# A search for a threshold: two small ScalarE operations of each step become one VectorE operation

## The chip, the cores and the metric

The kernel runs on one core of a Trainium2 chip. Five engines work side by side, each through its own queue in order: TensorE (PE, with its weight loads shown as PEld), VectorE (DVE), ScalarE (ACT), GpSimd (POOL) and SyncE (SP), which issues DMAs. An engine waits for another through semaphores; while the instruction at the head of a queue waits, everything behind it in that queue waits too. The metric is the device time of one execution in microseconds. Three runs of the kernel before gave 1814.0, 1814.33 and 1814.47 us; the median is 1814.33 us.

## What is computed

One transformer block over 1024 positions and a width of 1024: a mixer of two kinds of attention, a cross attention to a memory of 256 positions, and an MLP with a squared ReLU. The first kind of attention picks, for every query, the 256 keys with the largest index score, and attends only to these:

```python
idx_score = jnp.einsum('bqhs,bqh->bqs',
                       jax.nn.relu(jnp.einsum('bqhd,bsd->bqhs', qi, k_i)), wi).astype(jnp.float32)
idx_score = jnp.where(pos[None, None, :] <= t[None, :, None], idx_score, -jnp.inf)
_, sel = lax.top_k(idx_score, k_dsa)
kg = k_d[bidx3, sel]
vg = v_d[bidx3, sel]
s = jnp.einsum('bqhd,bqkd->bhqk', qd, kg).astype(jnp.float32) * ATTN_SCALE
p = _masked_softmax(s, (sel <= t[None, :, None])[:, None])
```

The second kind has three branches (compressed blocks, selected blocks, a sliding window), which are weighted by gates and summed. Everything behind the attention is dense: an output projection, the cross attention, and `square(relu(h @ w_ff_in)) @ w_ff_out`.

## The kernel before

The 1024 queries are eight tiles of 128. The first four tiles are projected alone. Then the attention of the eight tiles runs beside a stream of other work that keeps PE busy: the projection of the other four tiles, the memory's keys and values, and the output projection, cross attention and MLP of tiles that are ready. The last part, from about 1260 us, is the output side of the last tiles alone. `together` and `beside` interleave the generators by the estimated work that each yields; after that a scheduler of the tile framework puts the instructions of each engine in order by a timeline of its own and adds the semaphores. So the order on a queue isn't the order of the source, and an edit in one place can move instructions in others.

For tiles 2 to 7 (tiles 0 and 1 have no more than 256 keys) `index_mask` works one tile ahead of the attention. It computes the index scores (PE, with ReLU on ACT, L604, and the weighted sum on DVE, L608 and L610), and then looks for the 256th largest score of each query, which is each of the 128 partitions' own search. The scores' bits are mapped to two 16-bit halves, `hi` and `lo` (L618 to L620), whose order is that of the scores. The search goes bit by bit: 16 steps over `hi`, then 16 over `lo`, 32 steps a tile and 192 in all. A step of the kernel before has three instructions, all on ACT:

- L636: the sign of (key + threshold) for all keys of the row, 384 to 1024 wide by tile, with the sum of the signs written out to `over`. In the profile this is an ACTIVATE and an ACTIVATION_READ_ACCUMULATOR.
- L637: the sign of `over + need` for the one column, which tells if too many keys lie above the threshold.
- L638: the new threshold, `c - 0.5 * 2^b * step`, again one column.

Each needs the one before. As all three stand on the same engine, no other engine takes part in a step; the scheduler puts other ACT work between them. Between the halves DVE counts the keys above and zeroes the others (L631 to L634), and behind the search DVE rebuilds the threshold and writes the mask (L642 to L655), a chain of about ten instructions, the largest over the whole row. The mask `dmask` is what the score evictions of the first kind of attention add (L678).

Other lines that matter below: L235 (ACT) and L236 (DVE) copy a PSUM tile out in a rounded high part and the rest (`ph`, `pl`, `qh`, `ql`, `h`); L678 (DVE) evicts scores with the mask and the row's minimum `mn`; L680 (ACT) is the exponential; L685 (POOL) scales it; L244 (ACT) and L249 (POOL or DVE) split a weight tile from DRAM into `whi` and `wlo`; L401 (ACT) stages projected queries in `st`; L218 is every matmul of this form. In the changed file the lines from L642 on stand 2 lower down.

Of the kernel before, what the change touches and what calls it, by code (L numbers as in the profile page):

```python
# [9 lines left out]
F32 = mybir.dt.float32  # L10
# [6 lines left out]
AF = mybir.ActivationFunctionType  # L17
ALU = mybir.AluOpType
# [4 lines left out]
P = 128  # L23
# [5 lines left out]
BIG = 1e30  # L29
TOPK = 256  # L30
# [136 lines left out]
def build(nc, tc, I, C, out):  # L167
    v, s, g, te = nc.vector, nc.scalar, nc.gpsimd, nc.tensor
# [7 lines left out]
    at = at_pool.__enter__()  # L176
# [4 lines left out]
    def pst(tag, shape):  # L181
        return psum["pool"].tile(shape, F32, tag=tag, name="ps" + tag, bufs=psum["n"][tag],
                                 padded_shape=[P, 512 // int(np.prod(shape[2:]))] + list(shape[2:]))
# [33 lines left out]
    def mm(o, a, b, start, stop):  # L217
        te.matmul(o, a, b, start=start, stop=stop)  # L218

    def small(pool, tag, w, dt=F32, bufs=2, p=P):  # L220
        return pool.tile([p, w], dt, tag=tag, name=tag, bufs=bufs)
# [364 lines left out]
    def chunks_of(n):  # L586
        if n <= 4:
            return [(0, n)]
        a = (n + 1) // 2
        return [(0, a), (a, n - a)]  # L590

    def index_mask(aw, st, t):
        Wd = (t + 1) * P
        acc = small(aw, "isc", L, bufs=1)
        for hg in range(2):
            qh, ql = q_prep(aw, t, 2, hg)
            for h in range(4):
                for c, n in chunks_of(t + 1):
                    sp = pst("S", [P, n * P])
                    mv = st["K"][:, IDX, c * P:(c + n) * P]  # L600
                    mm(sp, qh[:, h, :], mv, True, False)
                    mm(sp, ql[:, h, :], mv, False, True)
                    r = small(aw, "ir", 512)
                    s.activation(r[:, :n * P], sp, AF.Relu)  # L604
                    dst = acc[:, c * P:(c + n) * P]
                    w = st["wi"][:, t, hg * 4 + h:hg * 4 + h + 1]
                    if hg == 0 and h == 0:
                        v.tensor_scalar(dst, r[:, :n * P], w, None, op0=ALU.mult)  # L608
                    else:
                        v.scalar_tensor_tensor(dst, r[:, :n * P], w, dst, op0=ALU.mult, op1=ALU.add)  # L610
                yield 0.15 * (t + 1)
        sc = acc[:, :Wd]
        v.tensor_tensor(acc[:, t * P:Wd], acc[:, t * P:Wd], causal[:, 384:512], op=ALU.subtract)
        bits = sc.bitcast(I16).rearrange("p (n b) -> p n b", b=2)
        mask = small(aw, "dmask", L, BF16)[:, :Wd]
        sgn = mask.bitcast(I16)
        hi, lo = small(aw, "tkh", L, U16, 1)[:, :Wd], small(aw, "tkl", L, U16, 1)[:, :Wd]
        v.tensor_scalar(sgn, bits[:, :, 1], 0.0, -1.0, op0=ALU.is_lt, op1=ALU.mult)  # L618
        v.scalar_tensor_tensor(hi.bitcast(I16), sgn, -32768, bits[:, :, 1], op0=ALU.bitwise_or, op1=ALU.bitwise_xor)
        v.tensor_tensor(lo.bitcast(I16), bits[:, :, 0], sgn, op=ALU.bitwise_xor)  # L620


        cnt, low = small(aw, "tkc", 1), small(aw, "tkf", 1)
        over, step, need = small(aw, "tko", 1), small(aw, "tks", 1), small(aw, "tkg", 2)
        th = small(aw, "tkt", 2)
        v.memset(need[:, 0:1], Wd - 2 * TOPK + 1.0)
        v.memset(th, 0.5 - 32768.0)
        for half, src in enumerate((hi, lo)):
            c, nd = th[:, half:half + 1], need[:, half:half + 1]
            if half == 1:  # L630
                v.tensor_scalar(low, th[:, 0:1], -1.0, None, op0=ALU.mult)  # L631
                v.tensor_scalar(mask, hi, low, None, op0=ALU.is_gt, op1=ALU.add, accum_out=cnt)
                v.tensor_scalar(nd, cnt, 2.0, Wd - 2 * TOPK + 1.0, op0=ALU.mult, op1=ALU.add)
                v.scalar_tensor_tensor(lo, hi, low, lo, op0=ALU.is_equal, op1=ALU.mult)  # L634
            for b in range(15, -1, -1):
                s.activation(mask, src, AF.Sign, bias=c, accum_out=over)  # L636
                s.activation(step, over, AF.Sign, bias=nd)  # L637
                s.activation(c, step, AF.Identity, scale=-0.5 * (1 << b), bias=c)  # L638
                yield 0.1
        ti = small(aw, "tki", 2, U32)  # L640
        tm, tb = small(aw, "tkm", 1, I32), small(aw, "tkb", 1, U32)
        v.tensor_scalar(ti, th, -1.0, None, op0=ALU.mult)  # L642
        v.scalar_tensor_tensor(tb, ti[:, 0:1], 16, ti[:, 1:2], op0=ALU.logical_shift_left, op1=ALU.bitwise_or)
        v.tensor_scalar(tm, tb.bitcast(I32), 31, None, op0=ALU.arith_shift_right)
        v.tensor_scalar(tm, tm, -1, -2147483648, op0=ALU.bitwise_xor, op1=ALU.bitwise_or)
        v.tensor_tensor(tb, tb, tm.bitcast(U32), op=ALU.bitwise_xor)
        thf = tb.bitcast(F32)
        eq = hi.bitcast(BF16)
        v.tensor_scalar(mask, sc, thf, None, op0=ALU.is_gt, op1=ALU.add, accum_out=cnt)
        v.tensor_scalar(cnt, cnt, -1.0, float(TOPK), op0=ALU.mult, op1=ALU.add)  # L650
        v.tensor_scalar(eq, sc, thf, None, op0=ALU.is_equal)
        v.tensor_tensor_scan(sc, eq, eq, 0.0, op0=ALU.add, op1=ALU.bypass)
        v.scalar_tensor_tensor(eq, sc, cnt[:, 0:1], eq, op0=ALU.is_le, op1=ALU.mult)
        v.tensor_tensor(mask, mask, eq, op=ALU.add)
        v.tensor_scalar(mask, mask, 1.0, -BIG, op0=ALU.subtract, op1=ALU.mult)  # L655
        st["dm"][t] = mask
        yield 0.1
# [169 lines left out]
    def attend(aw, st):  # L827

        main = attention(aw, st)
        held = []  # L830

        def of_tile(t):
            while True:
                x = held.pop() if held else next(main, None)
                if x is None:
                    return
                if x[0] > t:
                    held.append(x)
                    return
                yield x[1]  # L840
        for t in range(NT):
            if t + 1 in [a for a, _ in PARTS[1:]]:
                yield t, None
            side = index_mask(aw, st, t + 1) if 2 <= t + 1 < NT else iter(())
            for w in beside(of_tile(t), tile_work(t), side, 8 * 0.15 * (t + 2) + 3.4):
                yield t, w
        for x in main:
            yield x
# [204 lines left out]
    def pe_stack():  # L1053
# [10 lines left out]
    st = {  # L1064
        "K": at.tile([P, 6, L], F32R, tag="K", name="K"),
        "V": [at.tile([P, NT, 2, 2, 64], F32R, tag=f"V{b}", name=f"V{b}") for b in range(2)],
        "Vd": at.tile([P, NT, 2, 64], F32R, tag="Vd", name="Vd"),
        "Kc": {},
        "Vc": {},
        "cT": [at.tile([64, 2, 64], F32, tag=f"cT{kv}", name=f"cT{kv}") for kv in range(2)],  # L1070
        "cb": [at.tile([64, 1], F32, tag=f"cb{kv}", name=f"cb{kv}") for kv in range(2)],
        "wi": at.tile([P, NT, 8], F32, tag="wi", name="wi"),
        "gi": at.tile([P, NT, 24], F32, tag="gi", name="gi"),
        "dm": {},
        "ix": set(),
    }
    for kv in range(2):
        v.memset(st["cT"][kv], 0.0)
    pe = pe_stack()
# [8 lines left out]
    aw = aw_pool.__enter__()  # L1088
# [54 lines left out]
```

## Time and profile before

| | us |
|---|---|
| median of three runs | 1814.33 |
| the profiled execution's own time | 1807.76 |
| its span, first to last instruction | 1806.0 |
| PE busy | 1700.2 (94%) |
| PE weight loads busy | 1447.8 (80%) |
| DVE busy | 927.8 (51%) |
| ACT busy | 1061.9 (59%) |
| POOL busy | 887.4 (49%) |
| mean granted TensorE clock | 0.976 |
| L636 busy, with its read-out | 84.3 + 84.3 + 18.3 + 18.1 |
| L637 and L638 busy | 55.5 and 55.8 |

Busy time counts an engine's instructions from start to end, overlaps once. The ends of matmuls are modelled, so a busy PE isn't PE at its peak. A row of a group reads: line, engine, operation, output<-inputs, shapes, count, then busy us and mean ns of one, then the engine's idle time just before these instructions and who ended it. A wait is put down to the one that came last. A row of the timeline reads: start in us from the span's start, duration in us, engine, line, operation, and in brackets the engine's idle time just before. A row of one line's summary has min/median/max in ns behind the count, and first and last start in us.

The searches lie at 257 to 339, 364 to 441, 498 to 585, 664 to 764, 866 to 972 and 1097 to 1217 us, for tiles 2 to 7.

### The profile page before, as it was taken

The page shows a single profiled execution, that of the slowest core. Times are in us where ns is not written, and L with a number is a line of the kernel's source. Part 1 is how long each engine was busy: PE and PEld are TensorE (multiplying, and loading weights), DVE is VectorE, ACT ScalarE, POOL GpSimd, SP SyncE. Part 2 cuts the span into 40 slices and gives each one's busy share as a digit, 9 for nine tenths or more (in the row PEclk, how much of TensorE's full clock was granted, in tenths as well). Part 3 has the DMA queues.
Part 4 walks back from the last instruction along what each step waited for, and adds up shares of the span by engine and source line. Part 5 has one row for each costly group of instructions (what it writes and reads, how often), then busy time and mean ns, then how long its engine had stood idle before and what let it go on. Part 6 is the DMA issues. An engine that isn't in the chain of part 4 may idle for free. (4 is left out here: it accounts for less than half of the span.)

```text
span 1806.0 us, 27690 instructions
## 1 busy us (share of the span) xinstructions
PE 1700.2 (94%) x9134; PEld 1447.8 (80%) x9134; DVE 927.8 (51%) x2343; ACT 1061.9 (59%) x2655; POOL 887.4 (49%) x1015
## 2 busy tenths in 40 slices
PE   5987999899989999999998999999999799999998
PEld 5986888688878777788886888888888687787887
DVE  4545757665874776375754555646524322222221
ACT  4445669797688579855896558994513333333332
POOL 2356647363541355568575667662111144545444
PEclk9998999999999999999999999999999799999999
DMA  6235221366336211212122212226384122222222
GB/s 193 73 121 155 70 68 58 114 196 175 102 109 196 87 59 42 75 65 80 59 75 75 62 65 78 65 74 194 98 284 151 47 87 89 97 91 96 94 95 93
DMA packets 171887, 185.38 MB, mean 103 GB/s; under 512 B 26464, under 2 KB 140896, under 8 KB 171744
## 3 DMA queue, kind: packets, MB, share of 16 engines
q1 hardware_dynamic: 163808, 173.13, 30.3%
q0 software_dynamic: 7936, 10.49, 2.2%
q8 instruction: 72, 1.18, 0.3%
q14 instruction: 71, 0.58, 0.1%
HBM read 162.59 MB, written 20.97 MB: 102 GB/s over the span
## 5 line engine op out<-in xcount | busy, mean ns | idle before, releaser
L249 POOL TENSOR_TENSOR wlo<-wraw,whi 128x512 fp32r<-128x512 f32 (+1 forms) x231 | 310.6, 1351 | 280.9 <-ACT whi L244 252.9
L244 ACT ACTIVATE whi<-wraw 128x512 fp32r<-128x512 f32 (+2 forms) x289 | 181.0, 628 | 250.8 <-PE psS L218 156.8
L218 PE MATMUL psD<-whi,xh 128*128 128x256 f32 (+1 forms) x704 | 191.1, 352 | 4.4 <-ACT whi L244 3.4
L218 PE MATMUL psD<-wlo,xh 128*128 128x256 f32 (+1 forms) x704 | 190.3, 352 | 1.6 <-DMA wlo<-in_w_in_dram 1.0
L236 DVE TENSOR_TENSOR pl<-psPT,ph 128x512 fp32r<-128x512 f32 (+1 forms) x232 | 142.1, 621 | 78.9 <-ACT ph L235 76.3
L218 PE MATMUL psD<-whi,h 128*128 128x512 f32 x512 | 174.3, 403 | 3.7 <-ACT whi L244 1.6
L218 PE MATMUL psS<-whi,h 128*128 128x512 f32 x512 | 162.4, 392 | 5.4 <-DVE b L891 5.4
L680 ACT ACTIVATE S<-S,mn 128x128 f32<-128x128 f32 (+7 forms) x192 | 142.7, 744 | 40.5 <-DVE mn L678 39.0
L685 POOL TENSOR_SCALAR S<-S,sums,gi 128x640 f32<-128x640 f32 (+7 forms) x128 | 107.8, 853 | 114.1 <-DVE sums L683 103.5
L235 ACT ACTIVATE ph<-psPT 128x512 fp32r<-128x512 f32 (+1 forms) x232 | 122.9, 540 | 61.5 <-PE psPT L695 57.1
L249 DVE TENSOR_TENSOR wlo<-wraw,whi 128x512 fp32r<-128x512 f32 (+1 forms) x58 | 56.3, 971 | 170.3 <-ACT whi L244 170.1
L218 PEld LDWEIGHTS psD<-wlo,xh 128*128 128x128 f32 x704 | 132.4, 193 | 13.6 <-DMA wlo<-in_w_in_dram 1.4
L218 PEld LDWEIGHTS psD<-whi,xh 128*128 128x128 f32 x704 | 130.0, 193 | 14.2 <-ACT whi L244 3.8
L695 PE MATMUL psPT<-c_ident,S 128*128 128x128 f32 x816 | 131.8, 277 | 3.9 <-POOL S L685 2.6
L891 DVE TENSOR_TENSOR b<-psS,b 128x512 f32<-128x512 f32 (+1 forms) x80 | 49.9, 636 | 138.5 <-PE psS L218 138.5
L218 PE MATMUL psS<-K,qh 128*128 128x384 f32 (+3 forms) x288 | 112.4, 394 | 8.9 <-DVE mn L678 3.9
L218 PEld LDWEIGHTS psS<-whi,h 128*128 128x128 f32 x512 | 96.0, 188 | 30.4 <-DVE b L891 10.1
L218 PEld LDWEIGHTS psD<-whi,h 128*128 128x128 f32 x512 | 95.5, 189 | 25.8 <-ACT whi L244 2.0
L695 PEld LDWEIGHTS psPT<-c_ident,S 128*128 128x128 f32 x816 | 97.6, 142 | 14.1 <-POOL S L685 4.5
L218 PE MATMUL psD<-wlo,h 128*128 128x512 f32 x256 | 102.6, 404 | 1.1 <-POOL wlo L249 1.1
L218 PE MATMUL psD<-xh,wlo 128*128 128x512 f32 x256 | 101.5, 398 | 0.0
L891 DVE TENSOR_TENSOR b<-psD,b 128x512 f32<-128x512 f32 (+1 forms) x112 | 63.2, 573 | 74.0 <-PE psD L218 66.9
(289 smaller groups left out, 4546.2 us busy)
## 6 DMA issues: line engine op xcount, KB each, us to landing
wraw<-in_w_ff_in_dram SPq DMA_DIRECT2D x128, 256.0 KB, 2.7
wraw<-in_w_ff_out_dram SPq DMA_DIRECT2D x128, 256.0 KB, 2.6
whi<-in_w_out_dram SPq DMA_DIRECT2D x32, 256.0 KB, 3.8
wlo<-in_w_out_dram SPq DMA_DIRECT2D x32, 256.0 KB, 4.3
wraw<-in_w_in_dram SPq DMA_DIRECT2D x24, 256.0 KB, 3.4
q<-st SPq DMA_DIRECT2D x12, 512.0 KB, 2.6
qin<-q SPq DMA_DIRECT2D x44, 128.0 KB, 2.3
x<-in_x_dram SPq DMA_DIRECT2D x8, 512.0 KB, 5.5
```

The costliest lines, as they stand in the source:

```text
L218: te.matmul(o, a, b, start=start, stop=stop)
L235: s.activation(hi, src, AF.Copy)
L236: v.tensor_tensor(lo, src, hi, op=ALU.subtract)
L244: s.activation(hi, raw, AF.Copy)
L249: (v if l == "v" else g).tensor_tensor(lo, raw, hi, op=ALU.subtract)
L680: s.activation(S, S, AF.Exp, bias=low, scale=-1.0, accum_out=sums[:, hh:hh + 1])
L685: g.tensor_scalar(Ss[hh], Ss[hh], sums[:, hh:hh + 1], 1.0 if gate is None else gate[:, hh:hh + 1], op0=ALU.mult, op1=ALU.mult)
L695: te.transpose(p2[:, j, hh, :], S[:, (c + j) * P:(c + j + 1) * P], ident)
L891: v.tensor_tensor(dst, pt, dst, op=ALU.add)
```

## The change

L637 and L638 go from ACT, and one DVE instruction, a scalar_tensor_tensor with a sum over its columns written out, takes their place. It works on three columns: `over`, of which the first column is the sum of signs and the two others are a very large number, is compared with `need`, and the 0 or 1 is multiplied with a row of a table `tks` of the step: `-2^b`, the present threshold, and `0.5 * 2^b`. The large numbers always compare as greater, so the sum of the three products is the threshold, plus half of the bit, minus the bit if too many keys lay above. The sum is written to the middle column of the table's next row, from where the next step's L638 (the former L636) takes it as its bias; at the last step it goes to `th`. Table and `over` are now allocated once for the kernel and filled ahead of everything else with 34 column writes on DVE; before, `over`, `step` and `th` were small tiles in rings of two, and `th` was set for each tile.

```diff
-        over, step, need = small(aw, "tko", 1), small(aw, "tks", 1), small(aw, "tkg", 2)
+        over, tks, need = st["tko"], st["tks"], small(aw, "tkg", 2)
         th = small(aw, "tkt", 2)
-        v.memset(need[:, 0:1], Wd - 2 * TOPK + 1.0)
-        v.memset(th, 0.5 - 32768.0)
+        v.memset(need[:, 0:1], 2.0 * TOPK - 1.0 - Wd)
         for half, src in enumerate((hi, lo)):
-            c, nd = th[:, half:half + 1], need[:, half:half + 1]
+            nd = need[:, half:half + 1]
             if half == 1:
                 v.tensor_scalar(low, th[:, 0:1], -1.0, None, op0=ALU.mult)
                 v.tensor_scalar(mask, hi, low, None, op0=ALU.is_gt, op1=ALU.add, accum_out=cnt)
-                v.tensor_scalar(nd, cnt, 2.0, Wd - 2 * TOPK + 1.0, op0=ALU.mult, op1=ALU.add)
+                v.tensor_scalar(nd, cnt, -2.0, 2.0 * TOPK - 1.0 - Wd, op0=ALU.mult, op1=ALU.add)
                 v.scalar_tensor_tensor(lo, hi, low, lo, op0=ALU.is_equal, op1=ALU.mult)
             for b in range(15, -1, -1):
-                s.activation(mask, src, AF.Sign, bias=c, accum_out=over)
-                s.activation(step, over, AF.Sign, bias=nd)
-                s.activation(c, step, AF.Identity, scale=-0.5 * (1 << b), bias=c)
+                i = 15 - b
+                s.activation(mask, src, AF.Sign, bias=tks[:, i, 1:2], accum_out=over[:, 0:1])
+                v.scalar_tensor_tensor(small(aw, "tkj", 3), over, nd, tks[:, i, :], op0=ALU.is_gt, op1=ALU.mult,
+                                       accum_out=tks[:, i + 1, 1:2] if b else th[:, half:half + 1])
                 yield 0.1
...
+    st["tks"] = at.tile([P, 16, 3], F32, tag="tks", name="tks")
+    st["tko"] = at.tile([P, 3], F32, tag="tko", name="tko")
+    v.memset(st["tko"], BIG)
+    v.memset(st["tks"][:, 0, 1:2], 0.5 - 32768.0)
+    for i in range(16):
+        v.memset(st["tks"][:, i, 0:1], -1.0 * (1 << (15 - i)))
+        v.memset(st["tks"][:, i, 2:3], 0.5 * (1 << (15 - i)))
```

## The prediction

> **What bounds the kernel now.** I read the page's engine shares first, then the table of busy time cut at the first and last step of each of the six searches (tiles 2 to 7), then who made TensorE (PE) wait in those stretches.
>
> ```profile
> PE 1700.2 (94%) x9134; PEld 1447.8 (80%) x9134; DVE 927.8 (51%) x2343; ACT 1061.9 (59%) x2655; POOL 887.4 (49%) x1015
> ```
> ```profile
> core 0: us, PE busy (x) PEld busy (x) DVE busy (x) ACT busy (x) POOL busy (x), PEclk, DMA share, GB/s
> 257.00:339.00 82.00, 77.34 (x436) 65.61 (x436) 53.85 (x156) 74.03 (x258) 49.78 (x70) 0.98 0.21 64
> ...
> 364.00:441.00 77.00, 73.76 (x399) 65.80 (x400) 45.97 (x125) 70.26 (x213) 42.64 (x66) 0.94 0.65 188
> ...
> 498.00:585.00 87.00, 79.10 (x452) 69.17 (x450) 48.65 (x139) 77.36 (x210) 27.97 (x42) 0.98 0.47 147
> ...
> 664.00:764.00 100.00, 92.17 (x470) 74.37 (x471) 54.92 (x142) 91.80 (x228) 54.18 (x60) 0.97 0.17 54
> ...
> 866.00:972.00 106.00, 105.52 (x557) 89.18 (x556) 53.01 (x121) 98.93 (x232) 70.98 (x71) 1.00 0.25 77
> 972.00:1097.00 125.00, 119.60 (x605) 98.59 (x604) 80.80 (x172) 64.68 (x131) 81.12 (x79) 0.97 0.21 65
> 1097.00:1217.00 120.00, 120.00 (x654) 102.14 (x653) 63.32 (x170) 113.68 (x265) 82.49 (x86) 1.00 0.22 72
> ```
>
> PE sets the time: 94% busy. While a search runs, ScalarE (ACT) is the next fullest, 92% of the six stretches (526 of 572 us), VectorE (DVE) 56% (320 us). PE stands idle there for 4.7, 3.2, 7.9, 7.8, 0.5 and 0.0 us, 24.1 in all: that, with the clock dips beside it, is nearly all that a freer ACT can give. In the two longest searches PE never waits, though ACT is 93 to 95% full.
>
> Who ended PE's idle time in the first, third and fourth of these stretches (columns: waiter, awaited, us, times, longest):
>
> ```profile
> PE psD L218 <- ACT st L401: 1.9, 1, 1.9
> PE psPV L218 <- ACT tks L637: 1.0, 1, 1.0
> ...
> PE psPV L218 <- ACT ph L235: 0.6, 1, 0.6
> ```
> ```profile
> PE psM L274 <- DMA relu<-xo: 3.9, 1, 3.9
> PE psS L218 <- DVE mn L678: 1.0, 1, 1.0
> PE psPV L218 <- ACT ph L235: 1.0, 1, 1.0
> PE psM L274 <- ACT xh L278: 0.7, 1, 0.7
> ```
> ```profile
> PE psD L218 <- ACT whi L244: 1.6, 1, 1.6
> PE psS L218 <- DVE mn L678: 1.5, 2, 1.0
> ...
> PE psPV L218 <- ACT ph L235: 0.3, 1, 0.3
> ```
>
> ACT ended 1.9 + 1.0 + 0.6 + 1.0 + 0.7 + 1.6 + 0.3 = 7.1 us. The 3.9 us are a DRAM round trip of the memory attention, which no search touches.
>
> **What goes.** Of 192 steps, two ACT instructions each; the groups, then the timeline of ACT where steps stand alone and where another instruction stands between:
>
> ```profile
> L638 ACT ACTIVATE tkt<-tks,tkt 128x1 f32<-128x1 f32 x192 | 55.8, 291 | 3.0
> L637 ACT ACTIVATE tks<-tko,tkg 128x1 f32<-128x1 f32 x192 | 55.5, 289 | 2.3
> ```
> ```profile
> 501.00 0.28 ACT L637 ACTIVATE tks<-tko,tkg 128x1 f32<-128x1 f32 x1
> 501.19 0.37 ACT L235 ACTIVATE h<-psM 128x256 fp32r<-128x256 f32 x1
> ...
> 749.12 0.94 ACT L636 ACTIVATE dmask<-tkl,tkt 128x768 bf16<-128x768 uint16 x1
> 749.97 0.19 ACT L636 ACTIVATION_READ_ACCUMULATOR dmask<-tkl,tkt 128x1 f32 x1
> 750.18 0.29 ACT L637 ACTIVATE tks<-tko,tkg 128x1 f32<-128x1 f32 x1
> 750.51 0.29 ACT L638 ACTIVATE tkt<-tks,tkt 128x1 f32<-128x1 f32 x1
> 750.84 0.94 ACT L636 ACTIVATE dmask<-tkl,tkt 128x768 bf16<-128x768 uint16 x1
> ```
>
> Busy time falls by 55.8 + 55.5 = 111 us. From start to start a small one takes 0.19 us beside other work (501.00 to 501.19) and 0.33 in a bare chain (750.18 to 750.51), so ACT is really freed of 0.38 to 0.66 us a step, 73 to 127 us in all.
>
> **What comes.** One DVE instruction a step (L639 of the changed kernel: two SBUF tensors in, three columns, a running sum out). No row has just this form. The nearest: a one-column operation, an accumulator's read-out, a small operation with two SBUF tensors, and the two hand-overs between the engines:
>
> ```profile
> L633 DVE TENSOR_SCALAR tkg<-tkc x6: 132/146/149, 303.0 to 1158.6; 128x1 f32<-128x1 f32 x6
> ```
> ```profile
> L678 DVE DVE_READ_ACCUMULATOR2_ANT mn<- 128x1 f32 x256 | 20.8, 81 | 0.0
> ```
> ```profile
> L643 DVE SCALAR_TENSOR_TENSOR tkb<-tki x6: 159/160/1315, 339.1 to 1217.5; 128x1 uint32<-128x1 uint32 x6
> ```
> ```profile
> 972.29 1.31 POOL L249 TENSOR_TENSOR wlo<-wraw,whi 128x512 fp32r<-128x512 f32 x1
> 972.30 1.31 DVE L643 SCALAR_TENSOR_TENSOR tkb<-tki 128x1 uint32<-128x1 uint32 x1
> ```
> ```profile
> 506.25 0.20 ACT L958 ACTIVATION_READ_ACCUMULATOR relu<-psD,xnb,xsc 128x1 f32 x1
> ...
> 506.49 0.17 DVE L975 RECIPROCAL xsum<-xsum 128x2 f32<-128x2 f32 x1 [0.47 <-ACT relu L958]
> ```
> ```profile
> 346.31 0.08 DVE L678 DVE_READ_ACCUMULATOR2_ANT mn<- 128x1 f32 x1
> ...
> 346.43 0.62 ACT L680 ACTIVATE S<-S,mn 128x384 f32<-128x384 f32 x1 [1.67 <-DVE mn L678]
> ```
>
> Undisturbed it is 0.16 + 0.08 = 0.24 us, 46 us of DVE over 192 steps; lower end 0.15 without a read-out, 28 us; upper end 1.31 + 0.08 every time, 267 us. I take 0.24, and one in six held by GpSimd (POOL) as one of the six L643 was: 32 x 1.15 = 37 us more. DVE in the six stretches goes from 56% to about 71%, still more than a quarter free. A round trip with an empty DVE queue is 0.04 + 0.24 + 0.04 = 0.32 us (506.45 to 506.49, 346.39 to 346.43), half of the 0.66 it replaces.
>
> The new wait stands on both engines: each L638 on ACT waits for DVE, with PE's evictions (L235), the exponentials (L680, L682 in the changed file) and the weight casts (L244) queued behind it, for which PE waits; each L639 on DVE waits for ACT, with the score evictions (L678, there L680) and the low parts (L236) behind it. In the built order 33 of the 180 neighbouring steps have no ACT instruction between (39 before, small ones not counted) and 44 have one; the mean is 2.1, about 1 us of cover by rows like the 0.37 and 0.62 above. On DVE 3.3 instructions stand between two steps.
>
> The scheduler moves more than the two instructions: by the semaphores of the built order the six searches now lie over 2,054 places of PE's queue instead of 2,678. Counting for every wait of PE on ACT or DVE how many matmuls back the awaited instruction's own needs lie, waits with at most 8 matmuls of cover fall from 96 to 44 in the attention part (DVE 51 to 30, ACT 45 to 14), while those with at most 16 stay (383 and 385). No instruction on SP or POOL is added or removed.
>
> Thirty-four column writes are added ahead of everything on DVE, at 0.06 us each 2.0 us, and six removed. Cover: DVE there waits for the first loads anyway; without it they would cost their 2 us.
>
> ```profile
> L627 DVE MEMSET tkt<- x6: 60/60/60, 127.0 to 762.6; 128x2 f32 x6
> ```
> ```profile
> DVE qg L352 <- DMA qg<-in_nsa_qn_g_dram: 6.5, 1, 6.5
> ```
>
> **The sum.** (1) Of the 7.1 us of PE behind ACT, the 1.6 of whi stay, since that load was late too: -5.5. (2) Clock: the dips to 0.98, 0.94, 0.98 and 0.97 lose 1.6 + 4.6 + 1.7 + 3.0 = 10.9 us; in proportion to the idle time removed (5.5 of 23.6 us) -2.5. (3) Mask ready earlier. After the sixth tile's search DVE had sat behind its last step:
>
> ```profile
> 971.63 0.63 DVE L642 TENSOR_SCALAR tki<-tkt 128x2 uint32<-128x2 f32 x1 [16.68 <-ACT tkt L638]
> ```
>
> and in the stretch behind it (972 to 1097) PE loses 5.4 us. The mask's own operations still fill DVE then, so I take a little over a third: -2. (4) The new waits: the 37 us of held steps are mostly covered; DVE's 16.68 us above left PE with at most 0.5 us of idle in its own stretch and 5.4 in the next. I let a tenth through: +3.5. Sum -6.5. The profiled execution took 1807.76 us (span 1806.0), 6.6 us under the median 1814.33; it becomes 1801.3, the median **1807.8 us**.
>
> Bounds: for (1) to (3) together 0 to 27 (7.1 + 10.9 + 5.4, and 3.8 of clock at 0.97 in the stretch behind); for (4) 0 to 37.
>
> **Rivals.** (A) Slower: the hand-shake. ACT stood alone before; now a step advances only when both queues are there. Without cover a step costs 0.32 us plus half of a DVE operation under way (320 us over 853 instructions are 0.375 each, so 0.19) plus the mean hold of 37 / 192 = 0.19: 0.70, more than the 0.38 to 0.66 freed. It decides if the 77 steps with at most one instruction between lack cover: 77 x 0.70 = 54 us of late ACT, of which PE, without idle time in the last two searches so far, takes a quarter: +13.5 less the 2 of the mask, 1826 us. For it: ACT at 92% of the stretches, and shorter searches that pack it about as tightly. Against: fewer tightly covered waits, and PE at 100% with ACT at 95%. (B) No change: PE is full and ACT's idle time moves elsewhere; 1814 us. For it: 0.5 us of idle in the last 226 us of search. (C) L639 held by POOL whenever POOL works: it is busy 328 of the six stretches' 572 us, 57%; a half operation, 0.65 us, at 57% is 0.37 us a step, 72 us of DVE instead of 37. A tenth of it makes (4) +7 and the sum -3: 1811 us. The row is the L643 that ended with the POOL operation beside it. The Trainium skill says this as a rule ("SBUF — State Buffer", section "Who interferes with whom": a DVE instruction with two SBUF inputs contends with a GpSimd instruction that reads SBUF, and the second one waits); by that rule, C. The trace agrees in one of six.
>
> **Chances.** Forecast 0.50, A 0.34, B 0.09, C 0.07. Faster and slower by over 0.2% (3.6 us, about what a measurement of this kernel tells from no change): 0.50 and 0.35; within it 0.15. Range 1794 (three quarters of the 27 us) to 1827 (A, just within); the forecast alone 1797 to 1810.
>
> **What would show it.** Right: ACT busy near 950 us, L639 with its read-out near 0.24 us in the median and 60 to 100 us of DVE in all; PE's waits on st, tks and ph shorter; ACT's idle time put down to the new line well under the 111 us removed. Wrong: PE idle above 20 us in the last two searches, with ACT idle behind the new line (A); L639 mostly above 0.5 us (C).

## The result and the profile after

The changed kernel took 1829.76 us in the median of four runs (1823.37 to 1831.45), beside 1814.40 us (1814.00 to 1814.64) for the kernel before on the same chip: a ratio of 1.0091, 95% interval 1.0072 to 1.0111. It is slower by 0.9%, on the other side of the forecast and 3 us outside its range. The profiled executions are 1807.76 us (span 1806.0) before and 1823.37 us (span 1821.6) after, 15.6 us apart.

The engines' shares after the change, from the page:

```profile
PE 1707.0 (94%) x9134; PEld 1453.0 (80%) x9134; DVE 980.4 (54%) x2755; ACT 972.0 (53%) x2271; POOL 890.5 (49%) x1015
```

ACT is relieved of 89.9 us (1061.9 to 972.0), DVE gets 52.6. PE runs the same 9134 matmuls, and a change of its span is a change of its busy time, which grows when the granted clock is lower, plus a change of its idle time: 1707.0 - 1700.2 = 6.8 us more busy (clock 0.972, 0.976 before), and 114.6 - 105.8 = 8.8 us more idle. These are the 15.6 us.

The table by stages, cut at the first and last step of the searches for tiles 2 to 7, with one row more, between the searches of tiles 4 and 5:

```profile
core 0: us, PE busy (x) PEld busy (x) DVE busy (x) ACT busy (x) POOL busy (x), PEclk, DMA share, GB/s
257.00:313.00 56.00, 55.17 (x330) 48.55 (x329) 45.74 (x183) 48.19 (x161) 32.59 (x49) 1.00 0.25 69
...
364.00:421.00 57.00, 53.20 (x285) 46.28 (x284) 44.74 (x165) 49.54 (x138) 31.57 (x49) 0.90 0.58 158
...
496.00:564.00 68.00, 60.31 (x360) 52.17 (x359) 48.39 (x177) 55.37 (x136) 26.70 (x40) 0.97 0.42 128
564.00:652.00 88.00, 82.15 (x490) 70.67 (x489) 64.50 (x200) 45.21 (x115) 29.89 (x42) 1.00 0.40 120
652.00:736.00 84.00, 75.64 (x390) 65.42 (x391) 56.87 (x191) 71.42 (x155) 42.23 (x48) 0.86 0.14 39
...
840.00:922.00 82.00, 78.51 (x411) 65.04 (x412) 52.97 (x170) 70.41 (x143) 45.73 (x47) 1.00 0.22 64
...
1056.00:1142.00 86.00, 83.14 (x427) 69.89 (x428) 54.10 (x171) 75.89 (x148) 53.46 (x55) 0.98 0.23 68
```

From the start of the first large compare to the start of the last one, the six searches last 432 us in place of 550. (The six stretches above are 433 us; those of the prediction were cut a little wider, 572.) That part of the change works: a search is over sooner, and nothing is gained by it. In the shorter stretches PE is idle for 27.0 us (24.1 in the longer ones before), and the clock falls to 0.86 in the search of tile 5.

The new instruction itself, with what its engine waited for, and who waited for it:

```profile
L639 DVE SCALAR_TENSOR_TENSOR tkj<-tko,tkg,tks x192: 193/222/1251, 258.1 to 1143.0; 128x3 f32<-128x3 f32 x192
L639 DVE DVE_READ_ACCUMULATOR tkj<-tko,tkg,tks x192: 72/79/88, 258.4 to 1143.2; 128x1 f32 x192
```
```profile
L639 DVE SCALAR_TENSOR_TENSOR tkj<-tko,tkg,tks 128x3 f32<-128x3 f32 x192 | 62.7, 327 | 74.1 <-ACT dmask L638 73.2
```
```profile
DVE tkj L639 <- ACT dmask L638: 73.2, 88, 3.1
ACT dmask L638 <- DVE tkj L639: 28.3, 48, 2.2
```

It takes 222 + 79 = 301 ns in the median. The rows add up to 78 us; as the read-out starts before the row of the step has ended, DVE is occupied for 64.3. The steps that took longer than the median are 20.8 us above it in all. Most of that is holding by POOL: 54 steps took over 300 ns, and 52 of them ended within 0.1 us of the end of a POOL operation, while the 86 steps with no POOL operation beside them took 221 ns in the median. The longest step, with what POOL did (start, us, engine):

```profile
1068.85 1.30 POOL L249 TENSOR_TENSOR wlo<-wraw,whi 128x512 fp32r<-128x512 f32 x1
```
```profile
1068.92 1.25 DVE L639 SCALAR_TENSOR_TENSOR tkj<-tko,tkg,tks 128x3 f32<-128x3 f32 x1
```

ACT stood 28.3 us behind the step and DVE 73.2 us ahead of it, and DVE has the evictions for which PE waits in the same queue. PE's waits in the whole execution (waiter, awaited, us, times, longest):

```profile
PE psPV L218 <- DVE pl L236: 8.6, 13, 1.6
PE psS L218 <- ACT ir L604: 7.7, 3, 4.4
...
PE psPT L697 <- POOL S L687: 4.5, 5, 2.3
...
PE psPV L218 <- DVE oc L710: 2.7, 2, 1.7
```
```profile
PE psPV L218 <- DVE pl L236: 3.0, 8, 0.7
...
PE psPT L695 <- POOL S L685: 2.6, 5, 1.0
PE psS L218 <- ACT ir L604: 2.5, 3, 1.4
```

The second fence is the kernel before. Summed over all rows of this view, PE's waits on ACT fall from 23.0 to 18.5 us, those on DVE rise from 49.8 to 59.6, and those on POOL from 5.6 to 7.4.

Where the time is lost was read by laying the two traces over each other by the number of matmuls done. Up to 3,650 of them (about 655 us, the searches of tiles 2 to 4) the two stay within a few us. Between 3,650 and 4,100, in and just behind the search of tile 5, the changed kernel falls back by 13.4 us and gathers 4.7 us more idle time and 12.0 us more loss of clock. Most of this lag is gone again at 4,300 matmuls (4.3 us); it is 13.9 us at 6,500, behind the last search, and 15.6 at the end. The stretch of tile 5:

```profile
680.00:700.00 20.00, 15.46 (x74) 13.87 (x75) 16.72 (x55) 16.26 (x38) 10.02 (x16) 0.66 0.06 14
700.00:720.00 20.00, 18.17 (x83) 14.71 (x84) 14.36 (x42) 14.69 (x31) 9.43 (x10) 0.74 0.04 10
720.00:740.00 20.00, 20.00 (x99) 16.66 (x98) 8.80 (x31) 16.62 (x34) 13.87 (x15) 1.00 0.24 75
740.00:760.00 20.00, 16.33 (x64) 12.78 (x63) 15.24 (x31) 6.91 (x16) 9.90 (x9) 0.83 0.14 42
```

The last row is the mask's own work behind that search. In the timeline (start, us, engine) DVE's and POOL's long operations lie side by side, the index scores of the next tile (L608) come late by it, and PE waits:

```profile
742.09 2.72 POOL L1032 TENSOR_TENSOR h<-relu,h 128x512 fp32r<-128x512 f32 x1
743.78 1.85 DVE L655 SCALAR_TENSOR_TENSOR tkh<-isc,tkc,tkh 128x768 bf16<-128x768 f32 x1
...
747.12 2.16 DVE L608 TENSOR_SCALAR isc<-ir,wi 128x512 f32<-128x512 f32 x2
...
747.99 0.60 ACT L604 ACTIVATE ir<-psS 128x512 f32<-128x512 f32 x1 [5.13 <-DVE isc L608]
...
748.64 0.42 PE L218 MATMUL psS<-Kc,qh 128*128 128x64 f32 x1 [3.04 <-ACT ir L604]
```

So two accounts were open. Either the new operations cost this (the hand-shake of ACT and DVE, rival A), or the order does: the scheduler laid all five queues anew around a shorter search, and that order is worse.

### The profile page after: what moved, and what is told of

Read it like the earlier page. It is cut to its first block, busy times and chain, and to the rows that moved or that the text cites. A ratio compares the mean times of both kernels' runs of the same rounds, so it can differ in the third digit from the quotient of the medians.

```text
span 1821.6 us, 27669 instructions
## 1 busy us (share of the span) xinstructions
PE 1707.0 (94%) x9134; PEld 1453.0 (80%) x9134; DVE 980.4 (54%) x2755; ACT 972.0 (53%) x2271; POOL 890.5 (49%) x1015
## 5 line engine op out<-in xcount | busy, mean ns | idle before, releaser
L249 POOL TENSOR_TENSOR wlo<-wraw,whi 128x512 fp32r<-128x512 f32 (+1 forms) x231 | 314.4, 1367 | 298.4 <-ACT whi L244 252.2
L682 ACT ACTIVATE S<-S,mn 128x128 f32<-128x128 f32 (+7 forms) x192 | 142.8, 745 | 56.4 <-DVE mn L680 55.2
L236 DVE TENSOR_TENSOR pl<-psPT,ph 128x512 fp32r<-128x512 f32 (+1 forms) x232 | 141.4, 619 | 50.6 <-ACT ph L235 49.8
L687 POOL TENSOR_SCALAR S<-S,sums,gi 128x640 f32<-128x640 f32 (+7 forms) x128 | 112.3, 886 | 102.1 <-DVE sums L685 84.2
L249 DVE TENSOR_TENSOR wlo<-wraw,whi 128x512 fp32r<-128x512 f32 (+1 forms) x58 | 62.2, 1072 | 164.6 <-ACT whi L244 164.4
L218 PEld LDWEIGHTS psD<-wlo,xh 128*128 128x128 f32 x704 | 132.8, 193 | 13.9 <-DMA wlo<-in_w_in_dram 1.3
L218 PEld LDWEIGHTS psS<-whi,h 128*128 128x128 f32 x512 | 95.7, 188 | 30.8 <-DVE b L893 10.1
L639 DVE SCALAR_TENSOR_TENSOR tkj<-tko,tkg,tks 128x3 f32<-128x3 f32 x192 | 62.7, 327 | 74.1 <-ACT dmask L638 73.2
```

What stands on the lines that cost most here:

```text
L236: v.tensor_tensor(lo, src, hi, op=ALU.subtract)
L249: (v if l == "v" else g).tensor_tensor(lo, raw, hi, op=ALU.subtract)
L639: v.scalar_tensor_tensor(small(aw, "tkj", 3), over, nd, tks[:, i, :], op0=ALU.is_gt, op1=ALU.mult, accum_out=tks[:, i + 1, 1:2] if b else ...
L682: s.activation(S, S, AF.Exp, bias=low, scale=-1.0, accum_out=sums[:, hh:hh + 1])
L687: g.tensor_scalar(Ss[hh], Ss[hh], sums[:, hh:hh + 1], 1.0 if gate is None else gate[:, hh:hh + 1], op0=ALU.mult, op1=ALU.mult)
```

## Experiment 1: one kernel's operations in the other's order

Both kernels share all but the steps and their set-up: 8,266 PE instructions of the program (the page counts 9134), 1,973 DVE, 1,746 ACT, 1,011 POOL and 790 SP instructions correspond one to one. Each engine's shared instructions were chained in a given order, by dependencies that need no semaphore; what isn't shared finds its own place. No kernel was run held in its own order. The edit, shortened:

```diff
+def pin(nc, tc):
+    traced = {i.name: i for i in nc.cur_bb.bb.instructions}
+    for names in ORDER.values():          # one list for each engine
+        last = None
+        for name in names:
+            if last is not None:
+                tc.add_manual_dep(traced[name], last.name, NO_SYNC, reason="pin")
+            last = traced[name]
...
         build(nc, tc, I, C, out)
+        pin(nc, tc)
```

> The changed kernel's operations, with every instruction that the two kernels share (on all five queues) held in the order of the kernel before; only the 192 new VectorE steps and their set-up find their own place. Theory 1 (the operations themselves: the hand-shake between ScalarE and VectorE costs TensorE its time): the loss stays, 1824 to 1834 us. Theory 2 (the order: the shorter search let the scheduler lay the other work differently, and that order is worse): the loss goes, 1800 to 1816 us, with about 0.2 to 0.3 us still paid per VectorE step.

> The operations of the kernel before, with every shared instruction held in the order of the changed kernel; only the two small ScalarE operations of each step and two memsets find their own place. Theory 1 (operations): 1810 to 1818 us, as before. Theory 2 (order): 1826 to 1840 us, as slow as the changed kernel or slower, since that order was laid for steps without the two small operations.

New operations, old order: 1814.53 us, 1.0017 of the kernel before on the same chip (1.0007 to 1.0027). Old operations, new order: 1905.19 us, 1.0524 (1.0499 to 1.0549).

```profile
PE 1700.9 (94%) x9134; PEld 1447.1 (80%) x9134; DVE 985.1 (54%) x2755; ACT 977.8 (54%) x2271; POOL 885.7 (49%) x1015
```
```profile
DVE tkj L639 <- ACT dmask L638: 96.3, 96, 4.2
ACT dmask L638 <- DVE tkj L639: 29.8, 53, 2.2
```

With the old order the new operations lose 0.17%, not 0.91%, although ACT and DVE wait for each other at least as long as in the changed kernel (29.8 and 96.3 us). Of the 0.91, 0.74% or about 13 us comes with the order.

The other way round is a surprise in its size. 95 us over 192 steps are 0.49 us each, within the 0.38 to 0.66 us that the two small ACT operations were put at, so that little of them can be hidden. PE's waits there:

```profile
PE psPV L218 <- DVE pl L236: 14.3, 17, 3.6
PE psS L218 <- ACT ir L604: 12.3, 3, 6.1
...
PE psPV L218 <- ACT ph L235: 11.0, 9, 5.1
PE psD L218 <- ACT relu L1026: 8.2, 5, 3.1
```
```profile
PE 1738.7 (91%) x9134; PEld 1471.2 (77%) x9134; DVE 927.6 (49%) x2343; ACT 1074.7 (56%) x2655; POOL 887.2 (47%) x1015
```

Of 98.2 us between the spans (1904.2 and 1806.0), 59.7 are idle time of PE and 38.5 its longer busy time at a clock of 0.957. As I read it, an order laid for short steps has no room for long ones; in the order before, the same operations had their room.

## Experiment 2: the step left out

What would a step that costs nothing give? In each order the step was left out, and the search's large compare kept its place with a threshold that no longer moves. The first edit is to the kernel before, the second to the changed one:

```diff
-                s.activation(step, over, AF.Sign, bias=nd)
-                s.activation(c, step, AF.Identity, scale=-0.5 * (1 << b), bias=c)
```
```diff
-                v.scalar_tensor_tensor(small(aw, "tkj", 3), over, nd, tks[:, i, :], op0=ALU.is_gt, op1=ALU.mult,
-                                       accum_out=tks[:, i + 1, 1:2] if b else th[:, half:half + 1])
...
-        th = small(aw, "tkt", 2)
+        th = small(aw, "tkt", 2); v.memset(th, 0.5 - 32768.0)
...
-    v.memset(st["tks"][:, 0, 1:2], 0.5 - 32768.0)
+    v.memset(st["tks"][:, :, 1:2], 0.5 - 32768.0)
```

> The kernel before, its order held, with the two small ScalarE operations of every step left out and nothing in their place: the threshold no longer moves, so the masks are not the reference's. This is the whole of what a freer ScalarE can give in this order, with no hand-shake to pay. If terms (1) to (3) of the prediction are there to be had: 1796 to 1806 us. If TensorE is full and its idle time moves elsewhere (rival B): within 3 us of before, 1809 to 1815 us.

> The changed kernel, its order held, with the VectorE step left out and nothing in its place (the masks are not the reference's). If the new order is slow because it leaves too little cover for the step's round trip between ScalarE and VectorE (rival A, the hand-shake): the whole loss and more goes, 1795 to 1810 us. If the order is worse by itself, whatever a step costs: 1820 us or more.

Old order: 1803.34 us, 0.9964 (0.9952 to 0.9975), in the range for terms (1) to (3). New order: 1814.66 us, 1.0028 (1.0009 to 1.0047). With experiment 1 the ratios to the kernel before make a table:

| | no step | old step (ACT) | new step (DVE) |
|---|---|---|---|
| order of the kernel before | 0.9964 | 1 | 1.0017 |
| order of the changed kernel | 1.0028 | 1.0524 | 1.0091 |

At 1811 us to the whole: the old step costs 6.5 us in its own order; the new one 9.6 us (within about 3) in the old order and 11.4 (within about 5) in the new; the order costs 11.6 us without a step and 13.4 with the new one (within about 4 each). So the result is -6.5 (ACT freed) + 9.6 (the new step) + 13.4 (the order) = 16.5 us. The second expectation came true in neither of its forms: the step's share and the order's share are both there, and the intervals don't tell them apart in size.

What the new step does to PE is seen by comparing no step with the new step in one order. PE's waits on ACT rise from 18.4 to 22.9 us in the old order and from 15.4 to 18.5 in the new, although ACT's own work stays the same (976.6 and 977.8 us busy, 970.3 and 972.0). New on ACT is only its wait for the step on DVE, 29.8 and 28.3 us. PE's waits on DVE rise by less, 52.6 to 54.3 and 56.5 to 59.6. How much of the price is the waiting, and how much the 64 us for which the new step occupies DVE, these runs don't separate. In the old order PE's waits on ACT are then no shorter than before the change (22.9 beside 23.0 us): what the freed ACT gave, the hand-shake took.

What ACT's relief does and does not give is seen in two rows of the first of these kernels. The wait behind `st` stays (3.5 us before), so it wasn't the small operations that made it late; the wait behind `tks` (1.0) is gone.

```profile
PE psD L218 <- ACT st L401: 3.8, 2, 1.9
...
PE psPV L218 <- ACT ph L235: 1.5, 3, 0.8
```

## Experiment 3: the old order held for a part

If tile 5's search carries the loss, the old order up to and through it should bring the time back. The lists of experiment 1 were cut to what is traced ahead of a given step, 2,998 of the 8,266 PE instructions for tile 5 and 3,970 for tile 6. In outline (the names are not those of the file):

```diff
-    for names in ORDER.values():
+    for names in ([n for n in names if traced_before(n, FIRST_STEP_OF_TILE)] for names in ORDER.values()):
```

> The changed kernel's operations; what is traced ahead of the first step of tile 5's search (row tile 5, the fourth of six searches) is held in the order of the kernel before, the rest is left to the scheduler. If the loss lies in and behind tile 5's search, as the alignment of the two traces by TensorE's count has it: still 1824 to 1832 us. If it comes from the whole order in proportion, or from the first three searches: 1815 to 1822 us.

> The same with the old order held up to the first step of tile 6's search, so through the search of tile 5. If tile 5's search carries the loss (17 of 15.6 us between the two profiled executions, given back and lost again later): 1812 to 1819 us. If the loss is in the last two searches: 1824 us or more.

Held up to tile 5: 1823.49 us, 1.0075 (1.0051 to 1.0099), which lies between the two expectations. Held through tile 5: 1827.86 us, 1.0097 (1.0074 to 1.0121). My reading of the alignment falls. The first fence is the kernel whose order is held through tile 5, the second the new operations in the whole old order:

```profile
0.00:870.00 870.00, 793.62 (x4705) 692.91 (x4706) 577.20 (x1805) 537.70 (x1430) 442.00 (x587) 0.98 0.35 106
870.00:1075.00 205.00, 200.98 (x1055) 168.64 (x1054) 128.62 (x337) 139.14 (x284) 137.04 (x138) 1.00 0.21 68
1075.00:1430.00 355.00, 330.05 (x1751) 281.17 (x1750) 184.99 (x482) 172.57 (x353) 130.33 (x140) 0.96 0.40 126
1430.00:1822.40 392.40, 377.47 (x1628) 304.17 (x1626) 102.00 (x134) 124.67 (x206) 176.19 (x152) 0.99 0.27 88
```
```profile
0.00:870.00 870.00, 793.81 (x4703) 692.66 (x4704) 573.85 (x1804) 537.65 (x1428) 442.90 (x587) 0.98 0.36 106
870.00:1075.00 205.00, 198.54 (x1009) 164.68 (x1008) 125.51 (x317) 134.92 (x272) 133.26 (x135) 0.98 0.23 69
1075.00:1430.00 355.00, 342.34 (x1857) 295.94 (x1855) 191.17 (x512) 183.39 (x373) 134.61 (x144) 0.97 0.41 128
1430.00:1810.30 380.30, 366.21 (x1568) 293.86 (x1568) 94.57 (x125) 121.82 (x202) 174.89 (x150) 0.98 0.28 89
```

PE's two orders first part at 873 us, and up to there the two kernels are alike (4,705 and 4,703 matmuls). In the next 205 us, which hold the search of tile 6, the kernel that the scheduler is free in does 46 matmuls more. From 1075 to 1430 us, in the search of tile 7 and behind it, it does 106 fewer, with PE idle for 24.95 us in place of 12.66. So the stall at tile 5 is one form of the loss; take its order away, and as much is lost in the search of tile 7 and behind it.

## Experiment 4: other orders of the same operations

One constant of the plan, the share of work that a search counts for beside its attention tile, was changed in both kernels. The operations stay the same; where the steps are traced moves a little, and the scheduler does the rest.

```diff
-            for w in beside(of_tile(t), tile_work(t), side, 8 * 0.15 * (t + 2) + 3.4):
+            for w in beside(of_tile(t), tile_work(t), side, 8 * 0.15 * (t + 2) + 2.6):
```

> The kernel before with one constant of the plan changed, the share that a search is given beside its attention tile (3.4 becomes 2.6, so steps are traced later and closer together): the same operations in another order. If the order of the kernel before is an ordinary one among its neighbours: within 5 us of before, on either side. If it is an unusually good one, which any reshuffle loses, and the changed kernel lost it too: 1818 to 1830 us.

> The same with 3.4 become 4.6, steps traced earlier and further apart. Ordinary order: within 5 us of before. Unusually good order: 1818 to 1830 us.

> The changed kernel with the same constant at 2.6. If its order is an ordinary draw: 1815 to 1835 us, scattered about the changed kernel's 1826 to 1830. If shorter searches as such cost the time, whatever the arrangement: never under 1822 us.

> The changed kernel with the constant at 4.6. Ordinary draw: 1815 to 1835 us. Shorter searches as such: never under 1822 us.

> The kernel before with the plan's constant at 4.0. If the order of the kernel before is an unusually good one: slower than before by 5 to 30 us, 1816 to 1840. If the three orders so far were a poor sample: within 5 us of before.

> The changed kernel with the constant at 4.0. If the new step is no loss in an ordinary order (mean of ratios so far 1.006 for it, 1.008 for the old step): 1808 to 1832 us, and not slower than the old step at the same constant by more than the spread of the orders. If the new step is a loss of its own: slower than the old step at the same constant.

> The kernel before with the constant at 5.2. As at 4.0: 1816 to 1840 us if its own order is an unusually good one, within 5 us of before if not.

> The changed kernel with the constant at 5.2. Between 1805 and 1832 us if the order decides; a time under 1807 would make the changed step, with its plan set anew, faster than the kernel before by more than a measurement can miss.

Ratios to the kernel before, and the sums of PE's waits on ACT and on DVE in each profile (us):

| constant | old step | 95% | ACT / DVE | new step | 95% | ACT / DVE |
|---|---|---|---|---|---|---|
| 2.6 | 1.0147 | 1.0122 to 1.0172 | 30.8 / 54.3 | 1.0091 | 1.0068 to 1.0113 | 21.9 / 61.0 |
| 3.4 | 1 | | 23.0 / 49.8 | 1.0091 | 1.0072 to 1.0111 | 18.5 / 59.6 |
| 4.0 | 1.0064 | 1.0042 to 1.0086 | 37.3 / 53.1 | 1.0070 | 1.0042 to 1.0097 | 21.4 / 62.8 |
| 4.6 | 1.0081 | 1.0057 to 1.0106 | 31.4 / 51.4 | 0.9992 | 0.9977 to 1.0007 | 16.6 / 55.2 |
| 5.2 | 1.0109 | 1.0078 to 1.0140 | 25.2 / 57.8 | 1.0079 | 1.0048 to 1.0110 | 16.5 / 63.6 |

In times, the old step gives 1839.15, 1823.15, 1826.62 and 1831.69 us at 2.6, 4.0, 4.6 and 5.2, the new one 1827.50, 1824.08, 1811.52 and 1825.35, with the kernel before at 1811.4 to 1811.7 beside them. The 1811.52 also ends the idea that a shorter search costs the time in any arrangement: up to the end of the last large compare, the six searches last 435 us there and 438 in the changed kernel. The order of the kernel before is the best of the five by 0.6% and more: each reshuffle of its own operations loses 12 to 27 us, about as much as the change does or more. In the same five settings the change makes the time 0.56% shorter, 0.91% longer, 0.06% longer, 0.89% shorter and 0.30% shorter; the mean is -0.16% with a standard error of 0.31. Over five orders the new step is neither a gain nor a loss that these runs can show.

What the change does to PE's waits, with the scheduler free, has the same sign each time: those on ACT fall by 4.5 to 15.9 us (10.6 in the mean), those on DVE rise by 3.8 to 9.8 (7.2). At 4.0, the kernel with the old step first:

```profile
PE psD L218 <- ACT st L401: 7.5, 4, 2.1
PE psS L218 <- ACT ir L604: 6.2, 4, 3.6
...
PE psPV L218 <- DVE pl L236: 5.0, 10, 1.5
```
```profile
PE psPV L218 <- DVE pl L236: 6.9, 13, 1.2
...
PE psPV L218 <- ACT ph L235: 3.6, 7, 0.8
```

At 4.6 the changed kernel is level with the kernel before (1811.52 us beside 1811.42). No kernel in any setting was faster than the kernel before.

## Why the prediction was wrong

**The step that failed** is the paragraph that begins "The scheduler moves more than the two instructions". It counted PE's waits with little cover, found 96 before and 44 after, and gave the moved order no term in the sum and no end in the range. The order cost 11.6 to 13.4 us. The forecast change was -6.5 us and the measured one +16.5; of these 23.0 us the order is 13.4, and the terms (1) to (4) are the other 9.6. The count did not rank the two orders: the one with fewer closely covered waits is the slower one. The order before was the best of the five that were tried with its operations, which one trace of one kernel doesn't tell; that a new order may lose something should have been a rival with a price.

**Terms (1) to (3)**, -10 us together, were -6.5 (the step left out of the old order; interval -8.7 to -4.5). The sign was right and the size a third too large. In the two profiles PE's waits on ACT fall by 4.6 us (23.0 to 18.4), those on DVE rise by 2.8, and PE is idle for only 1.4 us less; the 1.9 us behind `st` were counted and stayed.

**Term (4)**, +3.5 us, was 9.6 in the old order and 11.4 in the new. I let it come from 37 us of steps held by POOL, with a tenth let through; 20.8 us of time above the median are there, a tenth of which is 2. What the term left out is the hand-shake: in both orders ACT stands 28 to 30 us behind L639 and DVE 73 to 96 us ahead of it, and PE's waits on ACT and on DVE are both longer with the step than without it (experiment 2).

**Rival A** had the side and nearly the size of the hand-shake (13.5 us; 9.6 to 11.4 measured) and so came close to the time, 1826. Its signs weren't there: it wanted over 20 us of idle PE in the last two searches, and there are 3.5 + 2.9 = 6.4. Its time came near by luck: the order, which it didn't have, made up the rest.

**Rival B**, no change because PE is full: refuted in its reason, since 6.5 us are to be had in the order before. **Rival C**, 72 us of holding by POOL: refuted in its size, by a median of 222 ns and the 20.8 us. Its mechanism is there, in more steps than the one in six that I took, and shorter in each. The Trainium skill ("SBUF — State Buffer", section "Who interferes with whom") states it as a rule: a DVE instruction with two SBUF inputs contends with a GpSimd instruction that reads SBUF. The trace agrees in 52 of the 54 steps over 300 ns. But of the 96 steps that began during a POOL operation only 51 took over 300 ns, and the runs don't tell why the others weren't held longer.

**The signs.** L639 at 60 to 100 us: 64.3, or 78 by its rows. Its median with the read-out at 0.24 us: 0.30. Waits on st, tks and ph shorter: in the changed kernel the first two are gone and ph falls from 2.3 to 0.5 us. ACT's idle time behind the new line well under 111 us: 28.3. ACT near 950 us: 972, since the small operations' rows overlap their neighbours and each took off 0.23 us (89.9 / 384), not 0.29. Nearly every local sign of the forecast came out, and the time went the other way: they all speak of the search, none of the rest of the kernel that was moved around it.

**Open.** The runs don't tell what makes the order before better than its neighbours. Stalls at tile 5, or in the search of tile 7 and behind it, are where two of the other orders lose; a single cause in all of them wasn't found. Nor is it known here whether the constant 3.4 had been chosen with the old step in place, which would favour the kernel before.

## What to carry to other kernels

Where a scheduler sets the order, an edit is two changes: the operations, and a new order of everything else. Hold the order to see the first, and reshuffle both versions by a constant of the plan to see the second; here a reshuffle of the kernel before alone costs 0.6 to 1.5%, and the edit in its fixed order 0.2%. Forecast such an edit with a term for the order that is as wide as that spread, and set the plan anew before an edit is judged: one other setting gave the whole 0.9% back.

## What the runs showed that I had not expected

- The same old operations cost 0.36% in an order laid around them, and 5.0% (1.0524 less 1.0028) in one laid for a shorter step: 90 us, 0.47 us a step. The six searches there, from the first large compare to the last, take 502 us in place of 414 without a step, so nearly all of it lies in the searches.
- Where small stalls cluster, the clock can cost PE more than the stalls do. In 680 to 720 us PE is idle for 6.4 us, and its granted clock is 0.66 and 0.74: the lower clock in these two rows is worth 6.8 + 5.2 = 12.0 us of full speed, nearly twice the idle time. That the stalls bring the clock down is my reading; no run here separates the two. The Trainium skill ("TensorE: Matmul & The Clock Gate", section "What's actually happening", the table of the states) says that PE falls to half its clock after an idle window of about 3.4 us; here the idle times that PE's rows show in 652 to 764 us are each at most 3.0 us, and the mean clock in the 20 us from 680 falls to 0.66 all the same.
- A DVE step that waits for ACT is paid by DVE's queue more than by ACT's: 73.2 us of DVE's waiting to 28.3 of ACT's, in an engine that is 54% busy, and PE's waits on DVE grew in all five settings.
